# Spare products between loads, and an early function table, in a router softmax

## The chip, the cores and the metric

The kernel runs on one core of a Trainium2 chip. The metric is the device time of one execution in microseconds (us). Before the change it is 85.58 us, the median of three runs (85.53 to 85.76).

## What is computed

A router: every row of x is multiplied by a small matrix, and a softmax is taken over the eight results.

```python
# x: (16, 512, 1024) float32, router_weights: (1024, 8) float32
logits = np.matmul(x, router_weights)
exp_logits = np.exp(logits - np.max(logits, axis=-1, keepdims=True))
return exp_logits / np.sum(exp_logits, axis=-1, keepdims=True)
```

x has 8192 rows of 4 KB, 33.55 MB in all. The output has 8192 rows of eight numbers, 0.26 MB.

## The kernel before

Each of the 128 partitions takes 64 consecutive rows of x. In the code and below, "row j" means the j-th row of every partition, so it is 128 rows of x at once. Rows are loaded in the groups of `LOADS`: four rows first, four loads of eight, four of four, three of two, five single rows, and row 63 in three pieces. The first four rows come as fp32, and ScalarE casts them; all others are cast to bf16 by the transfer.

For each row TensorE makes eight transposes of 128 x 128 ("turn": five into the buffer `ptv`, three into `pts`). VectorE copies the five out of the accumulation memory and ScalarE the three. Then TensorE multiplies the eight transposed pieces by the weights ("multiply"). Every eight rows, VectorE and ScalarE do the softmax. TensorE's loop handles two rows per round, and it begins each round with two products of a constant tile, `fill()`, whose result nobody reads; they keep TensorE at work.

```python
LOADS = [4] + [8] * 4 + [4] * 4 + [2, 2, 2] + [1] * 5
PIECES = [4, 2, 2]
TRIPS = 31
# ... cut ...
X_AT = place[0]                                # 16,640 bytes into a partition
xa = sb("x_all", [P, J, D], bf16)              # all 64 rows
x_f32 = sb("x_f32", [P, LOADS[0], D], fp32)    # rows 0 to 3 as loaded
# ... cut: GpSimd issues all loads but the first, one after the other, without a wait ...

def loop_turn(b):
    pe.wait_ge(s_in, 1).then_inc(s_in, -1)     # a row is there
    for c in range(KO):                        # 8 transposes
        ...                                    # reads at register r_x[c]
    for c in range(KO):
        pe.reg_add(r_x[c], r_x[c], D * 2)      # the next row
# ... cut ...
def fill():
    return pe.matmul(spare, lhsT=filler[:, 0:P], rhs=filler, start=True, stop=True)
# ... cut: weights, turn of row 0 ...
with nc.body("rows_multiply", valid_engines=only_pe):
    fill()
    fill()
    multiply(1, None)        # odd row of the round before
    pe.br("rows_turn")
with nc.body("rows_turn", valid_engines=only_pe):
    loop_turn(1)             # odd row
    multiply(0, None)        # the even row turned before it
    loop_turn(0)             # even row
    pe.br_lt(r_x[0], left_of(TRIPS - 1), on_true="rows_multiply", on_false="rows_done")
# ... cut: row 63 in its pieces, multiplications of the last rows ...

# ScalarE
act.wait_ge(s_f, 16).then_inc(s_f, -16)        # the first four rows are there
for i in range(2):
    cast(i)                                    # two rows, fp32 to bf16
    for j in (2 * i, 2 * i + 1):
        act_copy(j, j)
```

Of the kernel before, what the change touches and what calls it, by code (L numbers as in the profile page):

```python
# [11 lines left out]
def kernel(  # L12
# [6 lines left out]
    nc = tc.nc  # L19
    P = 128  # L20
    B, S, D = x.shape
# [10 lines left out]
    fp32 = mybir.dt.float32  # L32
    bf16 = mybir.dt.bfloat16
    Exp = mybir.ActivationFunctionType.Exp
    X = mybir.AxisListType.X
    ALU = mybir.AluOpType
# [3 lines left out]
    LOADS = [4] + [8] * 4 + [4] * 4 + [2, 2, 2] + [1] * 5  # L40
# [9 lines left out]
    assert sum(LOADS) == J - 1 and sum(PIECES) == KO and ends[-1] == J - ALONE  # L50
    VN, SN = 5, 3

    place = [16640]

    def sb(name, shape, dtype):
        size = mybir.dt.size(dtype)
        for n in shape[1:]:
            size *= n
        at = place[0]
        place[0] = -(-(at + size) // 64) * 64  # L60
        return nc.alloc_sbuf_tensor_at(name, shape, dtype, offset=at).ap()
# [1 line left out]
    def ps(name, shape, dtype):  # L63
        return nc.alloc_psum_tensor(name, shape, dtype).ap()

    X_AT = place[0]
    xa = sb("x_all", [P, J, D], bf16)
    x_f32 = sb("x_f32", [P, LOADS[0], D], fp32)
    identity = sb("identity", [P, P], bf16)
    ident = sb("ident", [P, P], fp32)  # L70
    w8 = sb("w8", [KO, P, N], fp32)
# [126 lines left out]
    pe = nc.tensor  # L198
    r_x = [pe.alloc_register(f"rx{c}") for c in range(KO)]
    r_l = pe.alloc_register("rl")  # L200
    for c, r in enumerate(r_x):

        pe.reg_mov(r, X_AT + D * 2 + c * P * 2 + (P - 1) * 2)
    pe.reg_mov(r_l, LG_AT + 256 * (SKIP - 1))

    def at(ap, like, r):
        return mybir.RegisterAccessPattern(
            ap=ap, dtype=like.dtype, memsetref=like.tensor.name + "_set",
            regref=r.name, is_regloc_offset=False, reg_ap_offset=r.name,
            const_ap_offset=0, const_sub_tensor_id=0,  # L210
        )

    def again(like, **k):
        return pe.add_instruction(copy.replace(like, name=f"I-{nc.next_id()}", **k))

    def turn_ap(b, c):
        return (ptv if c < VN else pts)[b][:, c if c < VN else c - VN, :]

    def chunk(b, c):
        return xTv[b][:, c, :] if c < VN else xTs[b][:, c - VN, :]  # L220

    def loop_turn(b):

        pe.wait_ge(s_in, 1).then_inc(s_in, -1)  # L224
        for c in range(KO):
            t = again(
                turn_like,
                ins=(turn_like.ins[0], at([[J * D, P], [1, P]], xa, r_x[c])),
                outs=(pe.lower_ap(turn_ap(b, c), opt=False),),
            )  # L230
            if c == VN - 1:
                t.then_inc(s_tv, 1)
            if c == KO - 1:
                t.then_inc(s_ts, 1)
        pe.reg_add(r_l, r_l, 256)
        for c in range(KO):
            if c == KO // 2:
                pe.reg_alu(r_l, r_l, -4097, ALU.bitwise_and)
            pe.reg_add(r_x[c], r_x[c], D * 2)
# [10 lines left out]
    def multiply(b, dst):  # L250

        for c in range(KO):
            if c == 0:
                pe.wait_ge(s_c[b], 2).then_inc(s_c[b], -2)
            if dst is None:
                m = again(
                    mult_like,
                    ins=(
                        pe.lower_ap(w_bf[:, c, :], opt=False),
                        pe.lower_ap(chunk(b, c), opt=False, for_matmul_weights=True),  # L260
                    ),
                    outs=(at([[2 * G * 64, P], [1, N]], lg, r_l),),
                    start_tensor_calc=(c == 0),
                    stop_tensor_calc=(c == KO - 1),
                )
            else:
                m = pe.matmul(  # L267
                    dst, lhsT=chunk(b, c), rhs=w_bf[:, c, :],
                    start=(c == 0), stop=(c == KO - 1),
                )  # L270
            if c == KO - 1:
                m.then_inc(s_p, 1)

    def fill():
        return pe.matmul(spare, lhsT=filler[:, 0:P], rhs=filler, start=True, stop=True)  # L275
# [17 lines left out]
    def left_of(i):  # L293

        return X_AT + D * 2 * (2 * i + 3) + (P - 1) * 2

    only_pe = OrderedEngineSet([pe.engine])
# [6 lines left out]
    with nc.body("rows_turn", valid_engines=only_pe):  # L304
        loop_turn(1)
        multiply(0, None)
        loop_turn(0)
        pe.br_lt(r_x[0], left_of(TRIPS - 1), on_true="rows_multiply", on_false="rows_done")
    nc.switch_bb("rows_done")
# [32 lines left out]
    act = nc.scalar  # L342
# [14 lines left out]
    def act_copy(j, seen):  # L357

        act.wait_ge(s_ts, seen + 1)
        act.copy(xTs[j % 2], pts[j % 2][:, 0:SN, :]).then_inc(s_c[j % 2], 1)  # L360

    act.wait_ge(s_f, 16).then_inc(s_f, -16)  # L362
    for i in range(2):
        cast(i)
# [181 lines left out]
```

## Time and profile before

| what | value |
|---|---|
| time, median of three runs | 85.58 us |
| span of the profiled run | 84.4 us |
| TensorE products, busy | 62.4 us (74%) in 1094 instructions |
| VectorE, busy | 39.4 us (47%) |
| ScalarE, busy | 38.0 us (45%) |
| GpSimd, busy | 11.3 us (13%) |
| memory read and written | 33.59 MB and 0.26 MB, 401 GB/s over the span |
| products of the constant tile (`spare`) | 61, of 512 columns, 19.6 us busy |
| function table load of ScalarE | 1, of 1.28 us |

The busy share of an engine is an average over the whole span, so it doesn't tell which engine sets the end. Products of TensorE are pipelined, and the sum of their durations counts stretches where several overlap only once. In the profile, `PE` is TensorE's products, `PEld` its weight loads, `PEq` its sequencer (a wait), `DVE` VectorE, `ACT` ScalarE and `POOL` GpSimd. The granted clock of TensorE is 1.00 at full speed. `ptv<-identity,x_all` is a turn; `lg<-w_bf,xTv` is a multiplication; `spare<-filler` is a fill. Line numbers are those of the kernel before.

### The profile page before, as it was taken

How to read it: one execution, taken by the hardware profiler on the slowest of the kernel's cores; microseconds unless marked ns; L12 is line 12 of the kernel's file. 1: busy time of each engine (PE TensorE's matmuls, PEld its weight loads, DVE VectorE, ACT ScalarE, POOL GpSimd, SP SyncE). 2: the span in 40 equal slices, each digit the busy share in tenths (PEclk: the TensorE clock that was granted, in tenths of full speed). 3: DMA queues.
4: the chain of work that ended last, by engine and by line, in shares of the span. 5: the costliest groups of instructions: out<-in, count | busy, mean ns of one | idle time of the engine just before them, and what ended most of it. 6: DMA issues, size and time to landing. Idle time of an engine off the chain costs nothing. (4 is left out here: it accounts for less than half of the span.)

```text
span 84.4 us, 2916 instructions
## 1 busy us (share of the span) xinstructions
PE 62.4 (74%) x1094; PEld 52.3 (62%) x1094; DVE 39.4 (47%) x114; ACT 38.0 (45%) x81; POOL 11.3 (13%) x26
## 2 busy tenths in 40 slices
PE   0070073999991999259990999999998799999870
PEld 0040072788871778238870688887887588777650
DVE  0030022247660685227660265678568357656662
ACT  0000988535460465225460254566546246546470
POOL 0699996000000000000000000000000000000000
PEclk9999999999999999999998579999999999999997
DMA  5999979997999799989998999999999999999930
GB/s 142 433 419 264 225 163 233 241 217 171 241 241 217 163 248 233 202 186 248 233 202 179 225 210 217 217 206 225 206 229 190 214 212 215 204 207 213 171 114 12
DMA packets 3184, 18.12 MB, mean 215 GB/s; under 512 B 488, under 2 KB 1000, under 8 KB 2032
## 3 DMA queue, kind: packets, MB, share of 16 engines
q0 software_dynamic: 2736, 15.73, 90.3%
q1 hardware_dynamic: 432, 2.36, 7.3%
q10 hardware_dynamic: 16, 0.03, 0.2%
HBM read 33.59 MB, written 0.26 MB: 401 GB/s over the span
## 5 line engine op out<-in xcount | busy, mean ns | idle before, releaser
L405 DVE COPY xTv<-ptv 128x640 bf16<-128x640 bf16 x63 | 31.0, 492 | 32.9 <-PE ptv L288 26.7
L360 ACT COPY xTs<-pts 128x384 bf16<-128x384 bf16 x63 | 30.1, 477 | 34.0 <-PE pts L288 33.6
L288 PE MATMUL ptv<-identity,x_all 128*128 128x128 bf16 x311 | 29.0, 226 | 14.4 <-PEq L224 9.5
L288 PEld LDWEIGHTS ptv<-identity,x_all 128*128 (+1 forms) x311 | 19.0, 99 | 15.4 <-issue 15.4
L288 PE MATMUL pts<-identity,x_all 128*128 128x128 bf16 x186 | 21.7, 228 | 0.0
L275 PEld LDWEIGHTS lg<-w_bf,xTv 128*128 128x128 bf16 x305 | 15.7, 98 | 7.9 <-issue 1.3
L275 PE MATMUL spare<-filler 128*128 128x512 bf16 x61 | 19.6, 402 | 0.2
L275 PE MATMUL lg<-w_bf,xTv 128*128 128x8 bf16 x305 | 16.7, 167 | 0.0
L288 PEld LDWEIGHTS pts<-identity,x_all 128*128 x186 | 13.9, 103 | 0.0
L275 PE MATMUL lg<-w_bf,xTs 128*128 128x8 bf16 x183 | 13.2, 166 | 0.0
L275 PEld LDWEIGHTS lg<-w_bf,xTs 128*128 128x128 bf16 x183 | 9.0, 96 | 0.0
L180 POOL DMA_DIRECT2D x_all<-in_x_dram x16 | 8.6, 588 | 2.2 <-POOLq L142 2.2
L275 PEld LDWEIGHTS spare<-filler 128*128 128x128 bf16 x61 | 4.7, 103 | 1.1 <-issue 1.0
L346 ACT ACT_TABLE_LOAD x1 | 1.3, 1283 | 8.5 <-ACTq L362 8.5
L282 PE MATMUL lg<-ident,w 8*128 8x8 f32 x8 | 1.0, 251 | 4.7 <-PEq L280 4.7
L346 ACT CAST x_all<-x_f 128x1024 bf16<-128x1024 f32 x4 | 4.0, 1044 | 0.0
L425 DVE TENSOR_REDUCE mx<-lg 128x8 f32 x8 | 1.8, 225 | 4.6 <-DVEq L475 4.1
L282 PEld LDWEIGHTS lg<-ident,w 8*128 8x128 f32 x8 | 0.9, 197 | 4.7 <-issue 4.7
L349 ACT ACTIVATE ev<-ex 128x64 f32<-128x64 f32 x8 | 2.1, 257 | 1.5 <-DVE ex L425 0.9
L396 DVE CAST identity<-ident 128x128 bf16<-128x128 f32 x1 | 0.5, 518 | 4.6 <-POOL ident L186 4.6
L441 DVE TENSOR_REDUCE ssum<-ev 128x8 f32<-128x64 f32 x8 | 1.7, 218 | 0.1
L425 DVE TENSOR_TENSOR ex<-lg,mx 128x64 f32<-128x64 f32 x8 | 1.7, 216 | 0.0
(41 smaller groups left out, 16.0 us busy)
## 6 DMA issues: line engine op xcount, KB each, us to landing
x_all<-in_x_dram POOLq DMA_DIRECT2D x4, 2048.0 KB, 27.7
x_all<-in_x_dram POOLq DMA_DIRECT2D x4, 1024.0 KB, 51.7
x_f<-in_x_dram SPq DMA_DIRECT2D x1, 2048.0 KB, 8.4
x_all<-in_x_dram POOLq DMA_DIRECT2D x3, 512.0 KB, 62.0
x_all<-in_x_dram POOLq DMA_DIRECT2D x5, 256.0 KB, 66.2
out_dram<-out_all SPq DMA_DIRECT2D x1, 240.0 KB, 2.0
x_all<-in_x_dram POOLq DMA_DIRECT2D x1, 128.0 KB, 67.8
x_all<-in_x_dram POOLq DMA_DIRECT2D x2, 64.0 KB, 67.5
```

The source lines that it names most:

```text
L180: nc.gpsimd.dma_start(out=xa[:, first[i]:first[i] + r, :], in_=x_rows[:, first[i]:first[i] + r, :]).then_inc(s_ld[i], 16)
L275: return pe.matmul(spare, lhsT=filler[:, 0:P], rhs=filler, start=True, stop=True)
L282: t = pe.transpose(w_ps[:, n, :], w8[:, :, n], ident[0:KO, 0:KO])
L288: turn_like = pe.transpose(turn_ap(0, 0), xa[:, 0, 0:P], identity).ins
L346: act.copy(xa[:, k, :], x_f32[:, k, :]).then_inc(s_cast, 1)
L349: return act.activation(ev, ex, func=Exp).then_inc(s_ev, 1)
L360: act.copy(xTs[j % 2], pts[j % 2][:, 0:SN, :]).then_inc(s_c[j % 2], 1)
L396: dve.tensor_copy(out=identity, in_=ident).then_inc(s_idb, 1)
L405: dve.tensor_copy(out=xTv[j % 2], in_=ptv[j % 2][:, 0:VN, :]).then_inc(s_c[j % 2], 1)
L425: return dve.add_instruction(kind(name=f"I-{nc.next_id()}", engine=dve.engine, **k))
L441: dve.reduce_sum(ssum[:, :, 0], ev, axis=X).then_inc(s_d, 1)
```

## The change

There are two parts. First, TensorE gets a third block in its loop. Behind the multiplication of the even row, a mask on the address register asks whether the next row is the first one behind a load of eight rows. If so, six fills are done before the wait for that row. They are meant to keep TensorE at work while it would wait for a load, so that its clock isn't lowered. For the mask to work on the address, the row buffer is moved to a round address, and the fp32 buffer for the first rows goes ahead of it. Second, ScalarE is told to load its function table ahead of its first wait, so that the load doesn't come between the arrival of the first rows and their cast.

```diff
+    LOT, SPARE = 8, 6
+    ROW_AT = 32 - LOADS[0] - LOT
+    assert LOADS[1:5] == [LOT] * 4 and 64 - ROW_AT == LOADS[0] + LOT * 5
...
-    X_AT = place[0]
+    x_f32 = sb("x_f32", [P, LOADS[0], D], fp32)
+    place[0] = X_AT = ROW_AT * D * 2
     xa = sb("x_all", [P, J, D], bf16)
-    x_f32 = sb("x_f32", [P, LOADS[0], D], fp32)
...
+    r_t = pe.alloc_register("rt")
...
         loop_turn(1)
         multiply(0, None)
+        pe.reg_alu(r_t, r_x[0], (64 + 32 + LOT - 1) * D * 2, ALU.bitwise_and)
+        pe.br_eq(r_t, 32 * D * 2, on_true="rows_spare", on_false="rows_even")
+    with nc.body("rows_spare", valid_engines=only_pe):
+        for _ in range(SPARE):
+            fill()
+        pe.br("rows_even")
+    with nc.body("rows_even", valid_engines=only_pe):
         loop_turn(0)
         pe.br_lt(r_x[0], left_of(TRIPS - 1), on_true="rows_multiply", on_false="rows_done")
...
+    act.preload_act_table(Exp)
     act.wait_ge(s_f, 16).then_inc(s_f, -16)
```

## The prediction
> **What bounds the kernel now.** I read the strip of forty slices first, for the DMA row, then the table of stages, cut at the moments where TensorE stops and starts. Columns of the stages: stretch, length, then busy time and count for PE, its weight loads, VectorE, ScalarE and GpSimd, then granted clock, DMA share, GB/s written.
>
> ```profile
> DMA  5999979997999799989998999999999999999930
> ...
> 17.30:27.10 9.80, 7.85 (x147) 6.74 (x144) 5.17 (x14) 4.46 (x10) 0.00 (x0) 1.00 1.00 214
> 27.10:36.80 9.70, 7.22 (x136) 6.04 (x136) 4.72 (x13) 3.98 (x9) 0.00 (x0) 1.00 1.01 216
> 36.80:46.50 9.70, 7.22 (x136) 6.04 (x136) 4.71 (x13) 3.98 (x9) 0.00 (x0) 0.97 1.01 215
> 46.50:49.50 3.00, 2.95 (x33) 2.42 (x34) 1.02 (x3) 0.48 (x1) 0.00 (x0) 0.52 1.04 218
> 49.50:65.20 15.70, 15.70 (x313) 13.49 (x309) 10.67 (x31) 9.23 (x22) 0.00 (x0) 1.00 1.03 214
> 66.00:79.60 13.60, 12.98 (x238) 10.65 (x238) 8.30 (x24) 6.89 (x16) 0.00 (x0) 1.00 1.10 208
> 79.60:84.40 4.80, 2.03 (x40) 1.67 (x40) 2.27 (x12) 2.06 (x7) 0.00 (x0) 0.91 0.27 70
> ```
>
> The reader is to see two things. The DMA share is 1.0 and the rate 208 to 218 GB/s in every stage up to 79.6, whether TensorE is busy 74% (7.22 of 9.70) or 100% of it, and whether its clock is 1.00 or 0.52. And TensorE has spare time in every stage but two: the stretch at half clock (46.5 to 49.5) and the one after it, where it works off the backlog. The bytes written are bf16, so the fp32 read is about twice that: a load of eight rows is 128 x 8 x 1024 x 4 = 4.19 MB, and 4.19 MB in 9.7 us is 432 GB/s.
>
> Next, the timeline of TensorE at the starts after a wait: start, duration, what, and in brackets the idle time before it.
>
> ```profile
> 14.62 0.69 PE L288 MATMUL ptv<-identity,x_all 128*128 128x128 bf16 x5 [1.45 <-PEq L224]
> ...
> 27.14 0.44 PE L288 MATMUL ptv<-identity,x_all 128*128 128x128 bf16 x5 [1.99 <-PEq L224]
> ...
> 36.88 0.44 PE L288 MATMUL ptv<-identity,x_all 128*128 128x128 bf16 x5 [2.48 <-PEq L224]
> ...
> 46.55 0.69 PE L288 MATMUL ptv<-identity,x_all 128*128 128x128 bf16 x5 [2.41 <-PEq L224]
> ...
> 66.02 0.44 PE L288 MATMUL ptv<-identity,x_all 128*128 128x128 bf16 x5 [0.81 <-PEq L224]
> ...
> 79.66 0.44 PE L288 MATMUL ptv<-identity,x_all 128*128 128x128 bf16 x5 [0.41 <-PEq L224]
> ```
>
> L224 is the wait for a row. The DMA issues, asked for one by one, give landings (issue + time to landing): loads 1 to 4 (rows 4, 12, 20, 28 onwards) at 17.3, 27.0, 36.7, 46.4; the four-row loads at 51.2, 56.1, 61.0, 65.8; row 62 at 11.8 + 67.7 = 79.5; the three pieces of row 63 at 80.1, 80.5, 80.9. Each start above but the first (ScalarE's casts hold that) lies 0.1 to 0.2 us behind a landing. So **the end is set by the transfers**: row 62 lands, and a chain of 4.8 us (79.6 to 84.4) follows: the last piece, transposed at 80.89, copies, products, softmax, and the store. The profiled run took 85.75 us for a span of 84.4.
>
> The duration 0.69 instead of 0.44 at 46.55 is the half clock: the wait of 2.41 us ahead of it let the clock fall, though the equal waits at 27.14 and 36.88 did not. The cold start shows the same 0.69 at 14.62.
>
> [...]
>
> **The change part by part.** *The table load.* Now ScalarE waits for the first rows and only then loads:
>
> ```profile
> 8.50 1.28 ACT L346 ACT_TABLE_LOAD   x1 [8.50 <-ACTq L362]
> 9.79 1.99 ACT L346 CAST x_all<-x_f 128x1024 bf16<-128x1024 f32 x2
> ```
>
> Moved ahead of the wait it lies in idle time, and casts, turns and copies of rows 0 to 3 begin 1.28 us earlier: row 0 at about 11.0 - 1.3 = 9.7, row 3's turn at 16.54 - 1.28 = 15.3. Row 4 is turned at 17.61 now and would be ready at 16.3, but its load lands at 17.3. So 0.2 to 0.3 us is gained there, a new wait of 1 us takes the rest, and row 12 waits for 27.0 in any case. At the end: 0.
>
> *The spare products.* TensorE's registers give the row number plus 20 (40,960 / 2,048 bytes), and the mask passes only 32, 40, 48 and 56: ahead of rows 12, 20, 28 and 36. One spare product of 512 columns takes 0.216 us at full clock (two fills, from 20.27 to the next product at 20.70, make 0.43) and 0.425 at half (15.43 to 16.28). Six take 1.30 us, four times make 24 products and 5.2 us. The first three lie in the waits: 1.99, 2.48 and 2.41 become about 0.7, 1.2 and 1.1 us. The rows still start at 27.1, 36.9 and 46.5, since they wait for landings.
>
> *The clock at 46.5.* With a wait of 1.1 us instead of 2.4 it should stay up. Now row 36's turn starts at 54.71, which is 8.16 us after row 28. Two rows with their two fills take 1.73 us at full clock (31.25 to 32.98), so eight would take 4 x 1.73 = 6.9, plus 0.2 behind a wait (36.88 to the fills at 37.53 is 0.65; with no wait, 38.82 to 39.26, it is 0.44): about 53.6. The half clock cost 1.1 us.
>
> *The fourth set* falls ahead of row 36, which landed at 51.2: TensorE is behind and waits for nothing, so its 1.30 us is added on TensorE's path: 53.6 + 1.3 = 54.9, against 54.7 now. The sum of the two is +0.2. From row 36 to row 48 are six pairs, 6 x 1.73 = 10.4: row 48 could start at 65.3, and it lands at 65.8. So TensorE waits there again, about 0.5 us instead of 0.8, and from there on nothing differs.
>
> *The mask and branch*, 31 times: [...] with one more jump in the four sets. They are sequencer work, beside the queued products; the last stands ahead of row 62's turn, inside the wait of 0.41 us. At the end: 0.
>
> *Memory.* The row buffer moves to byte 40,960 so that the mask works, and the fp32 rows go ahead of it; sizes, shapes and queues of the transfers are the same. I expect nothing.
>
> Sum on the path that sets the end: 0.
>
> **The rivals.** *(A) The warm clock brings time.* For it: 1.1 us is really lost after 46.5, and PE has the largest busy share on the page, 74%. Against it: that loss is made good before 65.2, where TensorE waits 0.81 us. If I misread that and TensorE bound the end, it would be 1.1 - 1.3 for the spare set, no gain either; only the table load could then show, 1.3 us: 84.3. *(B) The spare set ahead of row 36 delays the end.* If the clock fell all the same, row 36 would start at 56.0 and row 48 at 66.4, 0.6 us after landing. But rows come every 1.21 us (9.7 / 8) and TensorE needs 0.865 (1.73 / 2), so 0.35 is regained per row and 0.6 in two rows; the end stays. Only a second fall of the clock near the end would be seen, at up to 1 us by my estimate. Waits from 66 on are at most 0.41, so I don't expect it. *(C) The tail becomes longer*, through jumps or instruction fetching that can't hide between single rows: rows 60 to 62 start 0.1 us behind their landings. [...] *(D) The transfers themselves change*, by the new address or less contention. Their rate did not move between busy and idle stages (214 to 218), so I give this 0.3 us either way at most.
>
> **Range and chances.** The middle is the time before, less nothing: 85.55 us. The three runs of before spread 0.23 us; with (C) and (D) at 0.3 each way the range is 85.2 to 85.95. Faster by over 2% needs under 83.87, that is 1.7 us off a chain of transfers which the change doesn't touch: 0.02. Slower by over 2% needs over 87.3: 0.02. Within 2%: 0.96.
>
> **What would show it.** The table load should stand before 8.5 and the first cast at 8.5; row 0's turn near 9.7; a wait of about 1 us ahead of row 4; row starts at 27.1, 36.9 and 46.5 unmoved, with waits of 0.7, 1.2 and 1.1; no 0.69 at 46.5 and the clock row without its dip; 85 spare products instead of 61; row 48 at 66.0 behind a wait near 0.5; row 62 at 79.66 and the last chain of 4.8 us. The prediction is wrong if row 62 or the last piece lands more than 0.4 us away from where it does, if TensorE has no wait left ahead of row 48 nor of row 62, or if the clock falls after 66.

## The result, and the profile after

The changed kernel takes 87.09 us (median, 87.0 to 87.13), the kernel before 85.56 us beside it: a ratio of 1.0175, 95% interval 1.016 to 1.0191. It is slower by 1.5 us, outside the predicted range.

The stages, cut where those of before were cut (the last one longer, for the span is 85.7 us), with the same columns:

```profile
27.10:36.80 9.70, 9.07 (x144) 6.50 (x143) 4.70 (x13) 3.98 (x9) 0.00 (x0) 1.00 1.02 218
...
46.50:49.50 3.00, 2.92 (x48) 2.10 (x47) 2.00 (x6) 1.57 (x4) 0.00 (x0) 1.00 1.03 216
49.50:65.20 15.70, 15.43 (x271) 12.03 (x270) 8.29 (x24) 6.98 (x17) 0.00 (x0) 1.00 1.03 214
...
66.00:79.60 13.60, 13.29 (x239) 10.52 (x238) 7.98 (x23) 6.80 (x16) 0.00 (x0) 1.00 1.10 208
79.60:85.70 6.10, 3.18 (x66) 2.61 (x64) 3.33 (x17) 2.80 (x9) 0.00 (x0) 0.91 0.20 53
```

The spare products did what they are for: the clock is 1.00 from 46.5 to 49.5, where it was 0.52. The DMA share and rate up to 79.6 are those of before. But from 49.5 to 65.2 TensorE, called busy 15.43 of 15.70 us (products that overlap count once: over the whole run the 311 products of L296 into `ptv`, of 222 ns each, fill 28.3 us), got through 271 products where it had done 313. And the last stage has 66 products left instead of 40.

The timeline of TensorE, the starts behind a wait for a row, from row 4 on:

```profile
17.26 0.44 PE L296 MATMUL ptv<-identity,x_all 128*128 128x128 bf16 x5 [0.82 <-PEq L232]
26.96 0.44 PE L296 MATMUL ptv<-identity,x_all 128*128 128x128 bf16 x5 [0.44 <-PEq L232]
...
36.70 0.44 PE L296 MATMUL ptv<-identity,x_all 128*128 128x128 bf16 x5 [0.46 <-PEq L232]
46.37 0.44 PE L296 MATMUL ptv<-identity,x_all 128*128 128x128 bf16 x5 [0.42 <-PEq L232]
```

This is the whole list from row 4 on: behind 46.37 there is no wait any more. Rows 36 and 62 are turned here, at 54.71 and 79.66 in the kernel before:

```profile
55.48 0.44 PE L296 MATMUL ptv<-identity,x_all 128*128 128x128 bf16 x5
...
80.77 0.44 PE L296 MATMUL ptv<-identity,x_all 128*128 128x128 bf16 x5
```

Row 48 was turned at 67.08. The landings are not late: row 62 landed at 79.31 (79.49 before), the last piece at 80.67 (80.85). So **TensorE, no longer the transfers, sets the end**. The chain of work that ended last says the same, here for the kernel before and then for the changed one (share of the span by engine; before, the chain reaches back only to row 62 and its landing):

```profile
PE 2%; DVE 1%; ACT 0%; issue 0%
```

```profile
PE 39%; ACT 2%; DVE 1%; issue 1%
```

Why does TensorE need longer for the same products? Two stretches of the timeline show one round each: an even row's turn, the two fills of the next round, and the fills one round later. First before, then after.

```profile
58.16 0.44 PE L288 MATMUL ptv<-identity,x_all 128*128 128x128 bf16 x5
58.60 0.59 PE L275 MATMUL spare<-filler 128*128 128x512 bf16 x2
...
60.33 0.59 PE L275 MATMUL spare<-filler 128*128 128x512 bf16 x2
```

```profile
72.96 0.44 PE L296 MATMUL ptv<-identity,x_all 128*128 128x128 bf16 x5
73.24 0.33 PE L296 MATMUL pts<-identity,x_all 128*128 128x128 bf16 x3
73.61 0.61 PE L283 MATMUL spare<-filler 128*128 128x512 bf16 x2
...
75.57 0.60 PE L283 MATMUL spare<-filler 128*128 128x512 bf16 x2
```

A round is 60.33 - 58.60 = 1.73 us before, and 75.57 - 73.61 = 1.96 us after. From turn to fills it is 0.44 and 0.65 us. That 0.65 stood in the profile of before too, but only behind a wait; now it is in nearly every round. The waits of the weight loads count these gaps; each line is total us, times, longest, for before and for after:

```profile
PEld spare L275 <- issue: 1.0, 5, 0.2
```

```profile
PEld spare L283 <- issue: 6.1, 28, 0.3
```

"Issue" means that the engine waited for nothing that the profile shows. I read it as time in which its own sequencer had not yet handed over the next instruction. The sequencer's records, by line, give minimum, median and maximum in ns. The jump that ends a round, before:

```profile
L308 PEldq COMPARE_BRANCH  x31: 76/208/232, 15.0 to 80.0; - x31
```

The new mask and the new jump, after:

```profile
L315 PEldq ALU_OP  x31: 32/32/32, 11.5 to 80.3; - x31
L316 PEldq COMPARE_BRANCH  x31: 75/207/227, 11.7 to 80.4; - x31
```

The 75 ns are the four rounds (at 24.7, 34.4, 44.1 and 53.8) in which the jump is not taken and the program runs on into the spare products; in the other 27 it jumps over them, at 207 ns and more. What the two do to the sequencer is seen in the order of its records (start in us, from the trace, one round of each kernel, between the wait of a multiplication and that of the next turn):

```
before  59.322 wait L254                                                  59.473 wait L224
after   74.269 wait L262   74.419 mask L315   74.512 jump L316 (207 ns)   74.777 wait L232
```

That is 0.151 us before and 0.508 after, so the mask and the jump add 0.357 us. At the end of the round the sequencer of before has some time over: 0.195 us from the end of the jump (60.205) to its next wait record, against 0.078 in the changed kernel, so 0.117 us. My reading, theory S: the sequencer alone needs 1.727 - 0.117 = 1.61 us for a round, TensorE's products need 1.73, and 1.61 + 0.357 = 1.97 us is what a round then takes. The main rival, theory P: the products themselves are the cost, above all the set ahead of row 36, which lies in no wait.

### The profile page after: what moved, and what is told of

Its sections match the earlier page's. It is cut to its first block, busy times and chain, and to the rows that moved or that the text cites. A ratio compares the mean times of both kernels' runs of the same rounds, so it can differ in the third digit from the quotient of the medians.

```text
span 85.7 us, 3026 instructions
## 1 busy us (share of the span) xinstructions
PE 69.8 (81%) x1118; PEld 53.0 (62%) x1118; DVE 39.2 (46%) x114; ACT 37.9 (44%) x81; POOL 11.3 (13%) x26
## 5 line engine op out<-in xcount | busy, mean ns | idle before, releaser
L421 DVE COPY xTv<-ptv 128x640 bf16<-128x640 bf16 x63 | 30.9, 491 | 34.4 <-PE ptv L296 29.1
L296 PE MATMUL ptv<-identity,x_all 128*128 128x128 bf16 x311 | 28.3, 222 | 7.0 <-PEq L232 3.6
L283 PE MATMUL spare<-filler 128*128 128x512 bf16 x85 | 25.0, 391 | 1.3
L296 PEld LDWEIGHTS ptv<-identity,x_all 128*128 (+1 forms) x311 | 18.6, 98 | 9.3 <-issue 9.0
L296 PE MATMUL pts<-identity,x_all 128*128 128x128 bf16 x186 | 21.1, 224 | 0.0
L296 PEld LDWEIGHTS pts<-identity,x_all 128*128 x186 | 13.4, 100 | 0.0
L283 PEld LDWEIGHTS spare<-filler 128*128 128x128 bf16 x85 | 5.7, 98 | 8.0 <-issue 6.1
```

The costliest lines, as they stand in the source:

```text
L296: turn_like = pe.transpose(turn_ap(0, 0), xa[:, 0, 0:P], identity).ins
L421: dve.tensor_copy(out=xTv[j % 2], in_=ptv[j % 2][:, 0:VN, :]).then_inc(s_c[j % 2], 1)
```

## Experiments

**1. All the products, no mask and jump.** The loop is written out in five pieces, so that each set stands at its place without a mask and a jump. (Comments stand for the code that is left out.)

```diff
-        pe.reg_alu(r_t, r_x[0], (64 + 32 + LOT - 1) * D * 2, ALU.bitwise_and)
-        pe.br_eq(r_t, 32 * D * 2, on_true="rows_spare", on_false="rows_even")
+    for n, cut in enumerate(CUTS):     # a copy of the loop up to one round ahead of each set
...
+        # then that round written out, with SPARE fills between multiply(0) and loop_turn(0)
```

> All four spare sets stay, at the same rows, and so do the moved buffer and the early table; the loop is written out in five pieces, so that no mask and no conditional jump is needed to find the place of a set. Theory S (the sequencer: mask and jump lengthen TensorE's round from 1.73 to 1.96 us, and with the set ahead of row 36 the backlog is not made good): rounds of 1.73 us again, row 36 turned near 54.9, a wait ahead of row 48 and of row 62, time 85.4 to 85.8 us. Theory P (the spare products themselves are the cost): no better than the changed kernel, 86.9 to 87.2 us, rounds or row 62 as late as there.

Measured: 86.75 us against 85.67, 1.0116 (1.0095 to 1.0137). The time lies between what the two theories said, nearer to P, but the trace speaks for S. The starts behind a wait:

```profile
47.43 0.44 PE L296 MATMUL ptv<-identity,x_all 128*128 128x128 bf16 x5 [1.29 <-PEq L232]
...
67.10 0.44 PE L296 MATMUL ptv<-identity,x_all 128*128 128x128 bf16 x5 [0.80 <-PEq L232]
...
80.80 0.44 PE L296 MATMUL ptv<-identity,x_all 128*128 128x128 bf16 x5 [0.42 <-PEq L232]
```

TensorE waits again ahead of rows 28, 48 and 62, the last two times 0.80 and 0.42 us (0.81 and 0.41 before the change), with all 24 products in. The rows themselves came later: load 3 landed at 37.6 instead of 36.7, and row 62 at 80.6 instead of 79.5. The DMA queues of this run have a line that the others lack:

```profile
q8 instruction: 3, 0.05, 0.2%
```

Three packets of 16,384 bytes, at 31.3, 51.4 and 61.3 us, of 0.96 to 0.97 us each: by my reading blocks of TensorE's program, which is longer here. The DMA engines of load 3 finished over 1.3 us (36.30 to 37.61) instead of 0.8 (35.93 to 36.71), and its landing (37.6 instead of 36.7) is that of the last engine. So this kernel confounds its own test: fewer sequencer records per round, but later rows.

**2. The usual case falls through.** The block of spare products is moved ahead of the loop; nothing else changes.

```diff
+    with nc.body("rows_spare", valid_engines=only_pe):   # now ahead of rows_multiply
+        for _ in range(SPARE):
+            fill()
+        pe.br("rows_even")
     with nc.body("rows_multiply", valid_engines=only_pe):
...
-    with nc.body("rows_spare", valid_engines=only_pe):   # was between rows_turn and rows_even
```

> The changed kernel with the block of spare products moved ahead of the loop, so that the usual case falls through the conditional jump instead of taking it. In the changed kernel that jump takes 207 ns where it is taken and 75 ns in the four rounds where it falls through. Theory S: the jump takes 75 ns, the sequencer's round falls from 1.96 to about 1.61 + 0.22 = 1.83 us, row 36 near 55.1, row 62 ready near 79.0, ahead of its landing at 79.5: 85.4 to 85.9 us. Theory P: 87.1 us as the changed kernel. If it is any mask and compare, and not the jump, 86.9 to 87.1.

Measured: 85.67 us against 85.67, 1.0004 (0.9989 to 1.0018). The whole loss is gone, with all products, the mask and the jump in. The jump by line, and the starts at rows 48 and 62:

```profile
L320 PEldq COMPARE_BRANCH  x31: 75/75/207, 11.8 to 78.9; - x31
```

```profile
66.02 0.44 PE L296 MATMUL ptv<-identity,x_all 128*128 128x128 bf16 x5
...
79.47 0.44 PE L296 MATMUL ptv<-identity,x_all 128*128 128x128 bf16 x5 [0.40 <-PEq L232]
```

The median is 75 ns. Rounds take 1.85 us (rows 38 to 46), and 13 rounds from row 36 (55.11) bring TensorE to row 62 with 0.40 us to spare. Theory P is out: its products are all there. So are the early table and the moved row buffer, which therefore cost nothing that shows either.

**3 and 4. Two sets of the four.** The mask lets only rows 12 and 28 through, or only 20 and 36 (the first pair of lines is the edit for the former; the latter needs both).

```diff
-        pe.reg_alu(r_t, r_x[0], (64 + 32 + LOT - 1) * D * 2, ALU.bitwise_and)
+        pe.reg_alu(r_t, r_x[0], (64 + 32 + 8 + LOT - 1) * D * 2, ALU.bitwise_and)
-        pe.br_eq(r_t, 32 * D * 2, on_true="rows_spare", on_false="rows_even")
+        pe.br_eq(r_t, 40 * D * 2, on_true="rows_spare", on_false="rows_even")
```

> The changed kernel with a mask that lets only two of the four sets through, ahead of rows 12 and 28; mask and jump stay in every round. Both theories say that the set ahead of row 36 is needed for the loss. Theory S: rounds of 1.96 us, row 36 near 54.2, row 62 near 54.2 + 13 x 1.96 = 79.7, about at its landing: 85.5 to 85.9 us. A theory in which mask and jump alone cost the 1.5 us: 87.1 us.

> The counterpart: sets ahead of rows 20 and 36 alone, mask and jump in every round. Theory S: row 36 near 55.5 if the clock stays up at row 28 and about 1 us later if it falls in the wait ahead of it, row 62 at 81 to 82, 86.9 to 88.1 us. A theory in which it is the number of spare products (half of them here): 86.3 us.

Measured: 85.97 us for rows 12 and 28 (1.0028, 1.0017 to 1.004) and 86.99 us for rows 20 and 36 (1.0153, 1.0133 to 1.0174), against 85.67. In both, rounds take 1.95 us. Row 36 starts at 54.46 without its set and at 55.50 with it; row 62 at 79.88 and at 80.76. So with the long round the set ahead of row 36 costs 1 us, and the other sets nothing that shows: the place counts, not the number. The long round alone, with the clock up, costs 0.3 us: in the kernel with sets at rows 12 and 28, row 62 landed at 79.56 and started at 79.88, with no wait.

**5. The same as 1, in a shorter program.** One copy of the loop and one of the set's round are used for all four sets, and a second copy of the loop for the rest.

```diff
+        pe.br_lt(r_x[0], r_t, on_true="rows_multiply", on_false="rows_set")
+    with nc.body("rows_set", valid_engines=only_pe):
...      # the round with the set, written out
+        pe.reg_add(r_t, r_t, LOT * D * 2)
+        pe.br_lt(r_t, left_of(sum(LOADS[:6]) // 2 - 2), on_true="rows_multiply", on_false="rest_multiply")
```

> As the written-out loop (all four spare sets, no mask and no jump in the usual round), but with one shared copy of the loop and of the set's round, so that TensorE's program is about 420 instructions instead of about 1040. The written-out loop had rounds of 1.73 us and its waits back, but fetched three blocks of 16 KB of instructions during the run, each of which took 0.97 us on a DMA engine, and all landings from load 3 on came 0.9 to 1.1 us later. Theory S plus that fetch: no fetch now, landings where they were before, rounds of 1.73 us, waits ahead of rows 48 and 62, 85.5 to 85.9 us. If the fetch is not the cause: 86.7 us again, with late landings. If the spare products are the cost: 87 us.

Measured: 86.39 us against 85.59, 1.0101 (1.0078 to 1.0123). The expectation that nothing would be fetched was wrong:

```profile
q8 instruction: 1, 0.02, 0.1%
```

One block, at 31.0 us, of 0.95 us. Load 3 landed at 37.27 and row 62 at 80.03, each 0.55 us late. At row 62 that is half of the delay in experiment 1, which fetched three blocks; but there load 3 was already 0.9 us late behind its first block alone, so the delay doesn't simply go by their number. Rounds take 1.73 us, and the waits ahead of rows 48 (0.51) and 62 (0.34) are back, so what is left of the loss lies in the landings.

**6. Mask and jump, no products.** `SPARE` is 0.

```diff
-    LOT, SPARE = 8, 6
+    LOT, SPARE = 8, 0
```

> The changed kernel with no spare product in the sets; mask and jump stay in every round. Theory S: rounds of 1.96 us; row 36 near 54.2 and row 62 near 79.7 if the clock stays up in the longer waits, so 85.6 to 86.1 us; row 36 near 55.2 and row 62 near 80.7 if it falls at row 28, so 86.6 to 87.1. A theory in which the products alone cost: 85.6 us with rounds of 1.73.

Measured: 86.35 us against 85.59, 1.0081 (1.0052 to 1.011). That median stands between two groups of runs, as expected of either clock: nine of 85.6 to 85.9 us, with mean clocks of 0.970 to 0.995, and nine of 86.7 to 87.1 us, with 0.955 to 0.972 (one lies between, at 86.35). The profiled run is of the first group, and the clock fell in it at row 20, where it does no harm (stages, columns as above):

```profile
36.50:46.20 9.70, 8.80 (x136) 7.14 (x137) 4.66 (x13) 4.03 (x9) 0.00 (x0) 0.83 0.98 209
```

Turns take 0.69 us at 36.56 and 38.48, 0.52 at 39.55 and 0.44 from 40.70 on; a mean of 0.83 over 9.7 us is about 3.3 us at half clock. Even so those eight rows fit into the 9.7 us until the next load. Row 28 then starts at 46.23, row 36 at 54.06, row 62 at 79.39. No profile shows a run of the second group; that the clock falls at row 28 in it is inferred from the mean clocks, which overlap at 0.970 to 0.972, and is not shown. The first group (85.78 us in its middle, 0.2 more than before) and experiment 3 (0.3 more) say the same: the long round costs little as long as nothing else is added behind row 28. A set there adds 1 us (experiment 4); that a half clock there does so too would fit the second group.

**7. Sequencer work without a jump.** In the kernel before, four register operations that change nothing.

```diff
         multiply(0, None)
+        pe.reg_alu(r_l, r_l, -4097, ALU.bitwise_and)     # four times
         loop_turn(0)
```

> The kernel before, with four more register operations in each round (each repeats a mask on the output address that changes nothing), no jump, no spare set, no early table. Mask to jump take 0.093 us in the changed kernel's sequencer, so four are 0.37 us, about what mask and jump take together (0.36). Theory S: the sequencer's round is 1.61 + 0.37 = 1.98 us, and the time is that of the kernel with mask and jump but no products, 85.7 to 87.1 by the clock. A theory in which it is the jump itself that stops the queue: rounds of 1.73 and 85.6 us.

Measured: 86.74 us against 85.59, 1.0145 (1.0116 to 1.0174). Rounds take 1.97 us: row 28 at 46.19, row 36 at 54.07, row 62 at 79.68. No jump is needed: four register operations, whose records start 0.09 us apart and so make about 0.37 us, lengthen the round as mask and jump do. The time itself can't be compared with experiment 6, because a block of instructions was fetched at 82.9 us, in the last chain, which takes 5.32 us here instead of 4.76.

**8. The table load alone,** on the kernel before.

```diff
+    act.preload_act_table(Exp)
     act.wait_ge(s_f, 16).then_inc(s_f, -16)
```

> The kernel before with the early table load alone. All theories: first cast at 8.5 and row 0 near 9.7 instead of 11.0, a wait of about 1 us ahead of row 4, nothing at the end: 85.4 to 85.8 us, within 0.3% of before.

Measured: 85.6 us against 85.59, 1.0008 (0.9995 to 1.002). Row 0 is turned at 9.88 instead of 11.07, row 4 behind a wait of 0.66, row 12 at 26.91.

**9. All the products, no mask and jump, and no longer program.** A register holds the bound at which the loop stops, one round ahead of a set; the six fills are done between two rounds.

```diff
+    with nc.body("rows_set", valid_engines=only_pe):
+        for _ in range(SPARE):
+            fill()
+        pe.reg_add(r_t, r_t, LOT * D * 2)
+        pe.br_lt(r_t, SETS[3] + 1, on_true="rows_multiply", on_false="rows_last")
...
-        pe.br_lt(r_x[0], left_of(TRIPS - 1), on_true="rows_multiply", on_false="rows_done")
+        pe.br_lt(r_x[0], r_t, on_true="rows_multiply", on_false="rows_exit")
+    with nc.body("rows_exit", valid_engines=only_pe):
+        pe.br_lt(r_x[0], left_of(TRIPS - 1), on_true="rows_set", on_false="rows_done")
```

> All 24 spare products once more, without mask and jump in the usual round and without a longer program: the loop's own bound is a register that stops it one round ahead of each set, the six products are done between two rounds (two rows earlier than in the changed kernel), and the bound is moved on by eight rows. Early table and moved buffer stay. Theory S: no fetch of instructions, landings as before, rounds of 1.73 us, row 36 near 55, waits ahead of rows 48 and 62, 85.5 to 85.9 us, the same as before. If the products are a cost of their own: above 86.3.

Measured: 85.74 us against 85.6, 1.0017 (1.0008 to 1.0026). Nothing was fetched, rounds take 1.73 us, row 36 starts at 54.91, and the last starts behind a wait for a row are within 0.13 us of where the prediction had put those of the changed kernel (66.0 and 79.66):

```profile
65.88 0.44 PE L296 MATMUL ptv<-identity,x_all 128*128 128x128 bf16 x5 [0.47 <-PEq L232]
79.53 0.44 PE L296 MATMUL ptv<-identity,x_all 128*128 128x128 bf16 x5 [0.41 <-PEq L232]
```

This is the clean form of experiment 1: with 24 spare products, early table and moved buffer, the kernel is 0.14 us longer than before. The sets lie two rows earlier than in the changed kernel; experiment 2 has them at their own place.

**10. One register operation instead of four.**

```diff
         multiply(0, None)
+        pe.reg_alu(r_l, r_l, -4097, ALU.bitwise_and)     # once
         loop_turn(0)
```

> The kernel before with one more register operation in each round instead of four. Theory S: the sequencer's round is 1.61 + 0.09 = 1.70 us, still below the 1.73 us of the products, so rounds of 1.73 and 85.5 to 85.8 us, no difference. If every added sequencer operation lengthens the round: 1.82 us a round, and 86 us or more where the clock falls.

Measured: 86.5 us against 85.6, 1.0114 (1.0097 to 1.0131), where theory S had expected no difference. Inside the span there is none: row 48 starts at 65.80 behind a wait of 1.00, row 62 at 79.44 behind 0.41, and the span is 84.22 us. So one operation, of about 0.09 us, stays hidden, as the 0.117 us of slack had it. The loss is outside: 86.2 - 84.22 = 1.98 us, where the profiled runs of all the other kernels here have 1.32 or 1.33. A block of instructions was fetched at 85.5 us, after the last instruction of the span, for 0.93 us. That it makes up the missing 0.65 us fits, but was not tried apart.

No version beats the kernel before: the best ones end where the transfers end.

## Why the prediction was wrong, by its own steps

**What bounds the kernel:** right for before. Transfers set the end, and in experiments 2 and 9 they still do. What shows it is the trace, 208 to 218 GB/s in every stage up to 79.6, whatever TensorE did. What limits the transfers themselves was not shown.

**The table load:** right. First cast at 8.48, row 0 at 9.76, a wait of 0.82 ahead of row 4, nothing at the end (experiment 8).

**The spare products and the clock:** right in kind. The rows still start at 26.96, 36.70 and 46.37, and the clock stays up. The waits were predicted at 0.7, 1.2 and 1.1 us and are 0.44 to 0.46: rounds of 1.96 had eaten the rest, for with rounds of 1.73 in experiment 9 they are 1.01, 1.11 and 1.07.

**The mask and branch:** this is the step that failed: "They are sequencer work, beside the queued products", at a cost of 0 at the end. No measurement stood behind that, though the trace of before times a conditional jump: L308, with 208 ns in the median. The size of mask and jump was 0.357 us in the sequencer, from 0.032 for the mask, 0.207 for the jump and the steps between. The larger error was that the work had room beside the products. By theory S the sequencer was only 0.117 us per round from being the bound, so 0.24 us of the 0.357 went onto the path in each round: measured, 1.96 us a round instead of 1.73. One of the prediction's own signs of being wrong came with it: no wait is left ahead of row 48 or of row 62.

**The fourth set and the regaining:** right as long as a round is 1.73 us. Row 36 was put at 54.9 and started at 55.48, 0.58 late. Thirteen rounds to row 62 take 80.77 - 55.48 = 25.29 us instead of 13 x 1.73 = 22.5, so 2.8 more. By the prediction's numbers TensorE, had it never waited, would have been ready for row 62 at 54.9 + 22.5 = 77.4, or 2.26 us ahead of its start at 79.66 before. 0.58 + 2.8 - 2.26 = 1.1 us, and row 62 started 80.77 - 79.66 = 1.11 us late. The chain behind it is 4.91 us instead of 4.76. Together that is the 1.26 us between the two spans; the medians of all runs differ by 1.53.

**The rivals:** (B) named the right place, the set ahead of row 36, and dismissed it with 0.35 us regained per row. With 1.96 / 2 = 0.98 us per row it is about 0.23. (C) named jumps that can't hide, but in the tail alone, not in every round. Neither alone would have been enough: experiment 3, with the long round but no set ahead of row 36, loses 0.3 us; experiments 2 and 9, with the sets but rounds of 1.85 and 1.73, lose 0.14 us at most; both together cost the 1.5 us.

## What to carry to other kernels

TensorE's sequencer had a round of its own here, beside that of the products. Before adding a mask or a jump to a tight loop, add up the sequencer's records over a round and compare with the round of the engine's work; here 0.12 us was all the room there was. Lay out a block for the rare case so that the usual case falls through: here that took the jump from 207 to 75 ns and brought back the whole 1.5 us. And slack at one place (a wait of 0.41 us at the end, a backlog regained row by row) is shared: an extra cost per round and an extra cost once can each be free and together not be.

## What the hardware showed unexpectedly

- A conditional jump on TensorE's sequencer took 207 ns taken (the changed kernel, 27 rounds) and 75 ns not taken (its other four, and the median of experiment 2).
- A block of 16,384 bytes of instructions took 0.93 to 0.97 us of a DMA packet. During the loads, landings came 0.55 us (experiment 5, one block) or 0.9 to 1.1 us (experiment 1, three) later, and a block behind the last instruction went with 0.65 us more outside the span. No experiment varied the fetch alone. Why one added register operation led to a fetch, while the changed kernel, whose program is longer, had none, stays open.
- The clock fell at the end of waits as short as 1.74 us (experiment 7, row 20: turns of 0.69 us at 36.52 and 38.44, of 0.44 from 40.75 on) and stayed up through one of 2.48 us (the kernel before, row 20: turned in 0.44 us, with a clock of 1.00 up to 44.5).
